# Moving the low parts of the Strassen-stage weights from GpSimd to VectorE

## The chip, the cores and the metric

The kernel runs on one core of one Trainium2 chip. The metric is the device time of one execution in microseconds. Engine names in the rows: PE is TensorE (PEld its weight loads), DVE is VectorE, ACT is ScalarE, POOL is GpSimd, SP is SyncE, which issues nearly all DMAs.

## The reference, cut to what matters

One encoder block on a sequence of 1024 tokens of width 1024: a normalisation, one wide projection `h @ w_in` into twelve parts, a gated three-tap convolution mixer, a bidirectional delta-rule mixer, two gates, two output projections, a residual and a final normalisation. The change touches the part that computes five of the projected parts and multiplies them up:

```
proj = h @ w_in[l]
(a_bg, a_cg, a_x, a_z, q, k, v, z_b, a_raw, b_raw, gate_a_raw, gate_b_raw) = split(proj)
ya = a_cg * dwconv_centred(a_bg * a_x, conv_a_w[l])
ya = ya * jax.nn.silu(a_z)
...
merged = jax.nn.sigmoid(gate_a_raw) * ya + jax.nn.sigmoid(gate_b_raw) * yb
```

## The kernel before, in words

All large products are made in two parts: each float32 operand is written as a high part `hi` (rounded to TensorE's fast 32-bit type) and a low part `lo = x - hi`, and a product is hi·hi + hi·lo + lo·hi, three matmuls where one would do.

The stage of interest makes `a_bg`, `a_x`, `a_cg`, `a_z` (tiles named bg, ax, cg, az) and one pair of column blocks of gate b (gb). It takes the weight columns in pairs of 128-wide blocks, in the order bg, ax, cg, az, four times over, and then gb: 17 pairs. Each pair is a two-by-two block product done with seven products in place of eight (Strassen's scheme in Winograd's form). The seven are named by their weight operand: A11, A12, A22 are weight blocks as they were loaded (tiles `wr_...`), S1 to S4 are sums or differences of blocks (tiles `S_...`). One product is one **step** of the loop: 12 matmuls of 128x512. There are 17 × 7 = 119 steps, in the order S2, A11, S1, S3, A12, A22, S4 for all pairs but the first and the last.

Weights are prepared `AHEAD` = 5 steps before their product. `prep` (line 1203) makes the sum if there is one (VectorE, line 1194, behind the four DMA loads of the pair, line 1199, when it is the pair's first), then the high part (ScalarE, line 1206, tiles `whi..`, `wh..`), then the low part (GpSimd, line 1207, tiles `wlo..`, `wl..`). They go into six slots that are used in turn.

Behind each product stands `after`: VectorE and ScalarE take partial results out of PSUM. Three names matter. `e` is ScalarE's copy of the A11 product (line 1228). `u` (line 1230, VectorE) is the sum of a PSUM bank and `e`; it comes twice in a pair. The bank of pool `pg` first collects S2; the first `u` reads it behind A11, and only then may S3 be added into the same bank, so TensorE has one step (S1) between A11 and the product that waits. The second `u` reads the bank behind S3, and A22 is added only after it, with A12 between. In the first and the last pair the order differs, and A22 stands right behind S3.

In az pairs VectorE also multiplies the results up (line 1302 by c, line 1303 into `a`, between them ScalarE's silu of line 1294); the finished `a` is stored by SyncE (line 1305), behind which the loads of the next ax pair stand in SyncE's queue. In ax pairs line 1296 multiplies into `xpad`, and `conv3` (lines 1313 and 1315) runs the three taps, one a step.

Every engine works off its instructions in the order in which this code is written; an instruction that waits holds up all behind it on its engine.

Of the kernel before, what the change touches and what calls it, by code (L numbers as in the profile page):

```python
# [8 lines left out]
F32 = mybir.dt.float32  # L9
F32R = mybir.dt.float32r  # L10
AF = mybir.ActivationFunctionType
ALU = mybir.AluOpType
# [17 lines left out]
AHEAD = 5  # L30
# [278 lines left out]
def block(ctx: ExitStack, tc: tile.TileContext, x, c, wada, wadag, badaT, nwT, win, wab, cva, cvq,  # L309
# [3 lines left out]
    V, S, G, Q = (Engine(sched, n, e) for n, e in (("dve", nc.vector), ("act", nc.scalar), ("pool", nc.gpsimd),  # L313
                                                   ("dma", nc.sync)))
# [32 lines left out]
    def ch(c, w=P):  # L347
        return slice(w * c, w * c + w)
# [756 lines left out]
    V, S, G, Q, PE = nc.vector, nc.scalar, nc.gpsimd, nc.sync, nc.tensor  # L1105

    def bank(pl, name):
        return pl.tile([P, 512], F32, tag="b", name=name)
# [11 lines left out]
    def product(w, mhi, mlo, half, name, order=tuple(range(KT))):  # L1120
        ps = bank((pp, pg)[half], f"pp_{name}_{half}")
        for i, k in enumerate(order):
            wh, wl = (t[:, ch(i)] for t in w)
            sl = ch(half, 512)
            PE.matmul(ps, wh, mhi[k][:, sl], start=i == 0, stop=False)  # L1125
            PE.matmul(ps, wh, mlo[k][:, sl], start=False, stop=False)  # L1126
            PE.matmul(ps, wl, mhi[k][:, sl], start=False, stop=i == KT - 1)  # L1127
        return ps
# [38 lines left out]
    def slots(name):  # L1167

        i, place[0] = place[0], (place[0] + 1) % 6
        if i > 3:  # L1170
            return [bw.tile([P, 512], F32R, tag=p, name=f"w{p}{name}", bufs=2) for p in "hl"]
        if i % 2 == 0 or not spare:
            spare[:] = [wp.tile([P, KT * P], F32R, tag=f"w{p}", name=f"w{p}{name}") for p in ("hi", "lo")]
        return [t[:, ch(i % 2, 512)] for t in spare]

    class Pair:
# [26 lines left out]
        def prep(self, n):  # L1203
            t = self.operand(n if n in ADDS else (int(n[1]) - 1, int(n[2]) - 1))
            hi, lo = slots(f"{n}_{self.name}")
            S.activation(hi, t, AF.Copy)
            G.tensor_tensor(lo, t, hi.bitcast(F32), ALU.subtract)
            self.ops[n] = hi, lo

        def product(self, n):  # L1210
            own = (self.place, n) in (("first", "S4"), ("last", "A12"), ("last", "S4"))
            pl = po if own else BANK[n]
            first = own or pl not in self.banks
            if first:
                self.banks[pl] = bank(pl, f"ps_{self.name}_{n}")
            ps = self.banks[pl]
            hi, lo = self.ops.pop(n)
            for m in range(4):
                mh, ml = hop[RHS[n]][m]
                for i, (w, r) in enumerate(((hi, mh), (hi, ml), (lo, mh))):  # L1220
                    PE.matmul(ps, w[:, ch(m)], r, start=first and m == i == 0, stop=m == 3 and i == 2,  # L1221
                              skip_group_check=True)
            self.after(n, ps)
# [86 lines left out]
    def conv3(acc, b, j, i):  # L1310
        x, c = xpads[b][:, 1 + i : 1 + i + T], cva_t[:, j, i : i + 1]
        if i:
            V.scalar_tensor_tensor(acc, x, c, acc, ALU.mult, ALU.add)
        else:
            V.tensor_scalar(acc, x, c, None, ALU.mult)
# [21 lines left out]
    steps = [(p, n) for p in pairs for n in p.order]  # L1337

    def gate_block(j, w):
        xp = xpads[j % 2]  # L1340
        for half in range(2):
            ps = product(w, hhi, hlo, half, f"gb{j}", KORDER)
            S.activation(xp[:, 2 + 512 * half : 514 + 512 * half], ps, AF.Sigmoid)
        Q.dma_start(sgb_d[j], xp[:, 2 : T + 2])
# [3 lines left out]
    for i, j in enumerate(plain):  # L1348
        sums(i)
        if j + 1 in plain:  # L1350
            ws.append(wtile(win[G_B + j + 1], f"gb{j + 1}"))
        else:
            for p, n in steps[:4]:
                p.prep(n)
        gate_block(j, ws[i])
    for p, n in steps[4:AHEAD]:
        p.prep(n)
    hctx2.close()
    bt = sctx.enter_context(tc.tile_pool(name="bt", bufs=1, reuse_waits="tile"))
    for i, (p, n) in enumerate(steps):  # L1360
        if i + AHEAD < len(steps):
            q, k = steps[i + AHEAD]
            q.prep(k)
        p.product(n)
        if late:
            conv3(*late.pop(0))
        if i + 4 == len(steps):
            tctx.close()
            yp = ctx.enter_context(tc.tile_pool(name="yp", bufs=1, reuse_waits="tile", side="right"))
            yhi = [yp.tile([P, T], F32R, name=f"yhi{k}") for k in range(KT)]  # L1370
            ylo = [yp.tile([P, T], F32R, name=f"ylo{k}") for k in range(KT)]
            ws = [wtile(win[G_B + j], f"gb{j}") for j in (6, 7)]
            for k in range(KT):
                Q.dma_start(ylo[k].bitcast(F32), y_d[k])
# [204 lines left out]
```

## Time and profile before

| | |
|---|---|
| median of 3 runs | 1456.3 us (1455.89 to 1461.06) |
| the profiled execution: its own time | 1455.84 us |
| its span, first to last instruction | 1453.7 us (2.1 us lie around it) |
| TensorE busy over the span | 1379.9 us (95%) |
| VectorE, ScalarE, GpSimd busy | 828.2, 601.4, 664.9 us (57%, 41%, 46%) |
| mean granted TensorE clock | 0.986 |

How to read it: TensorE is busy for all but 5% of the span, so what another engine does counts where TensorE waits for it. The stage of pairs runs from about 824 to 1160 us of the span.

### The profile page before, as it was taken

What the parts mean: (1) busy time and instruction counts of PE and PEld (TensorE: products, weight loads), DVE (VectorE), ACT (ScalarE), POOL (GpSimd) and SP (SyncE); (2) the same over time, 40 slices, a digit from 0 to 9 for tenths busy, and PEclk for the clock granted to TensorE, in tenths of its full rate; (3) what the DMA queues carried; (4) which work ended last, traced back from release to release, by engine and by line L of the source; (5) the groups of instructions that cost most, each with busy time, mean ns of one, the idle gap of its engine ahead of it and who ended that gap; (6) DMA issues with size and microseconds to landing.
All of it is one profiled execution on the core that took longest, in us unless ns stands there. A gap on an engine that the chain in (4) does not pass through costs nothing.

```text
span 1453.7 us, 22475 instructions
## 1 busy us (share of the span) xinstructions
PE 1379.9 (95%) x8510; PEld 1151.7 (79%) x8510; DVE 828.2 (57%) x1377; ACT 601.4 (41%) x1487; POOL 664.9 (46%) x847
## 2 busy tenths in 40 slices
PE   6999979899989998999799999999999999999998
PEld 5777868787878787887688878787877788888886
DVE  7677165576666766677325556565657545422235
ACT  5437538474546474644443423232232342222211
POOL 2014736663936374757315644455445413355301
PEclk9999999999999999999899999999999999999999
DMA  9233341405050423314112410303030377665402
GB/s 366 75 109 98 99 105 44 131 30 147 15 153 22 107 69 80 96 34 113 44 44 88 145 55 18 116 16 116 29 116 30 123 273 256 207 203 179 179 15 101
DMA packets 123726, 154.41 MB, mean 106 GB/s; under 512 B 74593, under 2 KB 74977, under 8 KB 123618
## 3 DMA queue, kind: packets, MB, share of 16 engines
q1 hardware_dynamic: 123330, 152.19, 33.1%
q8 instruction: 67, 1.10, 0.3%
q10 hardware_dynamic: 288, 0.79, 0.1%
q14 instruction: 41, 0.34, 0.1%
HBM read 123.45 MB, written 29.50 MB: 105 GB/s over the span
## 4 chain that ended last, share of the span: by engine, by line
PE 68%; DVE 11%; DMA 7%; ACT 5%; POOL 4%; issue 3%; SPq 2%; POOLq 0%; ACTq 0%; DVEq 0%
PE cb L210 5%; PE pp_ga L210 5%; PE pp_v L210 4%; PE pp_z L210 3%; PE ps_ax_S L1221 3%; PE o L210 3%; PE ps_cg_S L1221 3%; PE ps_bg_S L1221 3%; PE pp_q L210 3%; PE ps_az_S L1221 2%; DVE N L303 2%; PE pp_pb L1125 2%; PE pp_pb L1127 2%; PE pp_pa L1127 2%; PE pp_pa L1125 2%
## 5 line engine op out<-in xcount | busy, mean ns | idle before, releaser
L303 POOL TENSOR_TENSOR E<-E,et 128x30 f32<-128x30 f32 (+7 forms) x240 | 116.7, 486 | 17.4
L303 POOL TENSOR_TENSOR et<-E 128x30 f32<-128x30 f32 (+7 forms) x240 | 111.3, 464 | 27.9 <-DMA E<-s 11.1
L303 DVE SCALAR_TENSOR_TENSOR S<-S,exps,cb 128x128 f32<-128x128 f32 x96 | 29.8, 344 | 60.2 <-PE cb L210 59.2
L303 ACT ACTIVATE vw<-cb,cols 128x128 f32<-128x128 f32 x112 | 36.2, 364 | 57.3 <-PE cb L210 57.1
L1117 POOL TENSOR_TENSOR wl_pa<-wr_pa,wh_pa 128x512 fp32r<-128x512 f32 x16 | 27.2, 1718 | 70.2 <-ACT wh_pa L1116 55.7
L303 POOL TENSOR_TENSOR wl_ga<-wr_ga,wh_ga 128x512 fp32r<-128x512 f32 x16 | 21.2, 1328 | 79.2 <-ACT wh_ga L303 60.1
L210 PE MATMUL pp_ga<-hhi,wh_ga 128*128 128x512 f32 x128 | 51.8, 404 | 3.4 <-ACT xpad L303 3.4
L303 POOL TENSOR_TENSOR wl_q<-wr_q,wh_q 128x512 fp32r<-128x512 f32 x14 | 18.2, 1304 | 78.8 <-ACT wh_q L303 78.8
L210 PE MATMUL pp_z<-hhi,wl_z 128*128 128x512 f32 x128 | 53.0, 414 | 0.0
L210 PE MATMUL pp_z<-hhi,wh_z 128*128 128x512 f32 x128 | 53.0, 414 | 0.0
L210 PE MATMUL pp_z<-hlo,wh_z 128*128 128x512 f32 x128 | 52.6, 411 | 0.0
L210 PE MATMUL pp_ga<-hhi,wl_ga 128*128 128x512 f32 x128 | 52.2, 408 | 0.0
L210 PE MATMUL pp_ga<-hlo,wh_ga 128*128 128x512 f32 x128 | 51.7, 404 | 0.0
L303 DVE SCALAR_TENSOR_TENSOR r<-cb,negeg,vp 128x128 f32<-128x128 f32 x112 | 34.6, 345 | 29.0 <-PE cb L210 28.2
L1125 PE MATMUL pp_pb<-bhi,wh_pb 128*128 128x512 f32 x128 | 50.4, 394 | 0.0
L1127 PE MATMUL pp_pb<-bhi,wl_pb 128*128 128x512 f32 x128 | 50.2, 392 | 0.0
L1126 PE MATMUL pp_pa<-ylo,wh_pa 128*128 128x512 f32 x128 | 49.8, 389 | 0.0
L1127 PE MATMUL pp_pa<-yhi,wl_pa 128*128 128x512 f32 x128 | 49.8, 389 | 0.0
L1125 PE MATMUL pp_pa<-yhi,wh_pa 128*128 128x512 f32 x128 | 49.8, 389 | 0.0
L1126 PE MATMUL pp_pb<-blo,wh_pb 128*128 128x512 f32 x128 | 49.7, 388 | 0.0
L303 DVE SCALAR_TENSOR_TENSOR qT<-xpad,cvq_t,qT 128x1024 f32<-128x1024 f32 x32 | 46.4, 1450 | 0.4
L210 PE MATMUL pp_v<-hhi,wh_v 128*128 128x512 f32 x112 | 46.4, 414 | 0.0
(802 smaller groups left out, 4603.2 us busy)
## 6 DMA issues: line engine op xcount, KB each, us to landing
wada<-in_wada SPq DMA_DIRECT2D x16, 512.0 KB, 8.9
D<-gr_d SPq DMA_DIRECT2D x16, 512.0 KB, 7.1
xt<-in_x SPq DMA_DIRECT2D x8, 512.0 KB, 9.0
wr_k<-in_win SPq DMA_DIRECT2D x16, 256.0 KB, 2.6
wr_q<-in_win SPq DMA_DIRECT2D x16, 256.0 KB, 3.7
wr_v<-in_win SPq DMA_DIRECT2D x16, 256.0 KB, 3.4
wr_ga<-in_win SPq DMA_DIRECT2D x16, 256.0 KB, 3.3
qg<-er_d SPq DMA_DIRECT2D x8, 512.0 KB, 6.5
```

What stands on the lines that cost most here:

```text
L210: getattr(self.pe, what)(out, *ins, **kw)
L303: self._sched.record(self._name, lambda: real(*args, **kw), outs, ins, cost, extra, table, op == "memset", port)
L1117: G.tensor_tensor(lo[:, ch(q, 512)], raw, hi[:, ch(q, 512)].bitcast(F32), ALU.subtract)
L1125: PE.matmul(ps, wh, mhi[k][:, sl], start=i == 0, stop=False)
L1126: PE.matmul(ps, wh, mlo[k][:, sl], start=False, stop=False)
L1127: PE.matmul(ps, wl, mhi[k][:, sl], start=False, stop=i == KT - 1)
L1221: PE.matmul(ps, w[:, ch(m)], r, start=first and m == i == 0, stop=m == 3 and i == 2, skip_group_check=True)
```

## The change: what it does

`prep` no longer makes the low part. A new method `rest` makes it on VectorE, with the same operands, and is called one step later than `prep` of the same operand: at step i the loop first prepares step i + 5 and then calls `rest` for step i + 4, ahead of the product of step i.

```diff
             S.activation(hi, t, AF.Copy)
-            G.tensor_tensor(lo, t, hi.bitcast(F32), ALU.subtract)
-            self.ops[n] = hi, lo
+            self.ops[n] = hi, lo, t
+
+        def rest(self, n):
+            hi, lo, t = self.ops[n]
+            V.tensor_tensor(lo, t, hi.bitcast(F32), ALU.subtract)
...
-            hi, lo = self.ops.pop(n)
+            hi, lo, _ = self.ops.pop(n)
...
-            for p, n in steps[:4]:
+            for s, (p, n) in enumerate(steps[:4]):
                 p.prep(n)
+                if s:
+                    steps[s - 1][0].rest(steps[s - 1][1])
         gate_block(j, ws[i])
-    for p, n in steps[4:AHEAD]:
-        p.prep(n)
+    for i in range(4, AHEAD):
+        steps[i][0].prep(steps[i][1])
+        steps[i - 1][0].rest(steps[i - 1][1])
...
         if i + AHEAD < len(steps):
             q, k = steps[i + AHEAD]
             q.prep(k)
+        if i + AHEAD <= len(steps):
+            q, k = steps[i + AHEAD - 1]
+            q.rest(k)
         p.product(n)
```

VectorE's queue between the second `u` of an az pair and the first `u` of the bg pair behind it, before (the second of the three places where az is followed by bg looks the same but for numbers; this is the third):

```order
L1230 TENSOR_TENSOR u_az_10064<-ps_az_S_9985,e_az_10017 128x512
L1291 TENSOR_TENSOR t_az_10066<-ps_az_S_10035,u_az_10064 128x512
L1302 TENSOR_TENSOR t_az_10066<-t_az_10066,c_9926 128x512
L1303 TENSOR_TENSOR a_9817<-t_az_10066,a_9817 128x512
L1302 TENSOR_TENSOR t_az_10085<-t_az_10085,c_9945 128x512
L1303 TENSOR_TENSOR a_9836<-t_az_10085,a_9836 128x512
L1194 TENSOR_TENSOR S_bg_10089<-wr_bg_10025,wr_bg_10021 128x512
L1291 TENSOR_TENSOR t_az_10107<-ps_az_S_9985,e_az_10017 128x512
```

The same place in the changed kernel, up to the same instruction, two rows longer:

```order
L1233 TENSOR_TENSOR u_az_10063<-ps_az_S_9984,e_az_10016 128x512
L1294 TENSOR_TENSOR t_az_10065<-ps_az_S_10034,u_az_10063 128x512
L1305 TENSOR_TENSOR t_az_10065<-t_az_10065,c_9925 128x512
L1306 TENSOR_TENSOR a_9816<-t_az_10065,a_9816 128x512
L1211 TENSOR_TENSOR wloA_bg_10048<-wr_bg_10024,whiA_bg_10047 128x512
L1305 TENSOR_TENSOR t_az_10084<-t_az_10084,c_9944 128x512
L1306 TENSOR_TENSOR a_9835<-t_az_10084,a_9835 128x512
L1194 TENSOR_TENSOR S_bg_10088<-wr_bg_10024,wr_bg_10020 128x512
L1211 TENSOR_TENSOR wloA_bg_10048<-S_bg_10028,whiA_bg_10047 128x512
L1294 TENSOR_TENSOR t_az_10106<-ps_az_S_9984,e_az_10016 128x512
```

The rest of that stretch in the changed kernel, up to the first `u` of bg and on to the second one:

```order
L1305 TENSOR_TENSOR t_az_10106<-t_az_10106,c_9925 128x512
L1306 TENSOR_TENSOR a_9816<-t_az_10106,a_9816 128x512
L1211 TENSOR_TENSOR wlS_bg_10091<-S_bg_10088,whS_bg_10090 128x512
L1294 TENSOR_TENSOR t_az_10128<-ps_az_S_10034,u_az_10018 128x512
L1305 TENSOR_TENSOR t_az_10128<-t_az_10128,c_9944 128x512
L1306 TENSOR_TENSOR a_9835<-t_az_10128,a_9835 128x512
L1211 TENSOR_TENSOR wlA_bg_10113<-wr_bg_10026,whA_bg_10112 128x512
L1194 TENSOR_TENSOR S_bg_10151<-wr_bg_10026,S_bg_10030 128x512
L1211 TENSOR_TENSOR wloA_bg_10135<-wr_bg_10022,whiA_bg_10134 128x512
L1233 TENSOR_TENSOR u_bg_10170<-ps_bg_S_10138,e_bg_10168 128x512
L1194 TENSOR_TENSOR S_ax_10180<-wr_ax_10172,wr_ax_10174 128x512
L1194 TENSOR_TENSOR S_ax_10182<-S_ax_10180,wr_ax_10176 128x512
```

Behind these stand two more low parts and then the second `u`, which before the change followed the two sums of ax directly:

```order
L1211 TENSOR_TENSOR wloA_bg_10135<-S_bg_10151,whiA_bg_10134 128x512
L1211 TENSOR_TENSOR wloS_ax_10185<-S_ax_10182,whiS_ax_10184 128x512
L1233 TENSOR_TENSOR u_bg_10215<-ps_bg_S_10138,e_bg_10168 128x512
L1288 TENSOR_TENSOR xpad_116<-ps_bg_S_10188,u_bg_10215 128x512
L1211 TENSOR_TENSOR wloS_ax_10185<-wr_ax_10176,whiS_ax_10184 128x512
```

What moved: 119 rows of line 1207 left GpSimd's queue and stand, as line 1211, in VectorE's, seven to a pair. In the stretch shown five of them come between the second `u` of az and the first `u` of bg (four ahead of the sum `S_bg_10151`, one behind it), and two between the sums of ax and the second `u` of bg. Apart from these, the order on TensorE and ScalarE is as before; on SyncE one store and one load behind the stage change places.

## Rows read from the trace of the kernel before

**Rows 1.** Busy time of the engines in the stage (819 to 1150 us): start and end, length, busy time (instructions) of PE, PEld, DVE, ACT, POOL; then TensorE's granted clock, DMA share, GB/s. The second row is the same for the instructions of line 1207 alone, all of them on POOL.

```profile
819.00:1150.00 331.00, 326.26 (x1406) 262.73 (x1405) 203.29 (x222) 95.45 (x164) 166.46 (x120) 1.00 0.20 67
819.00:1150.00 331.00, 166.09 (x119) 1.00 0.20 67
```

**Rows 2.** TensorE's timeline at the places in the stage where it stood still: start us, duration us, engine, line, operation, out<-in, and in brackets the idle time before it with what ended it. Matmuls overlap, so their starts, not their durations, give the pace.

```profile
841.49 0.47 PE L1221 MATMUL ps_bg_S<-T4h,whiS_bg 128*128 128x512 f32 x1 [0.88 <-DVE u_bg L1230]
...
872.55 0.50 PE L1221 MATMUL ps_cg_S<-T3h,whiS_cg 128*128 128x512 f32 x1 [0.33 <-DVE u_cg L1230]
...
911.12 0.39 PE L1221 MATMUL ps_bg_S<-T1h,wloA_bg 128*128 128x512 f32 x1
912.38 0.50 PE L1221 MATMUL ps_bg_S<-T3h,whiS_bg 128*128 128x512 f32 x1 [0.88 <-DVE u_bg L1230]
912.72 0.39 PE L1221 MATMUL ps_bg_S<-T3l,whiS_bg 128*128 128x512 f32 x1
...
990.66 0.51 PE L1221 MATMUL ps_bg_S<-T3h,whiS_bg 128*128 128x512 f32 x1 [0.47 <-DVE u_bg L1230]
...
996.06 0.40 PE L1221 MATMUL ps_bg_A<-hhi,wloS_bg 128*128 128x512 f32 x1
996.48 0.53 PE L1221 MATMUL ps_bg_S<-T4h,whiA_bg 128*128 128x512 f32 x1
996.84 0.40 PE L1221 MATMUL ps_bg_S<-T4l,whiA_bg 128*128 128x512 f32 x1
...
1069.23 0.50 PE L1221 MATMUL ps_bg_S<-T3h,whS_bg 128*128 128x512 f32 x1 [0.45 <-DVE u_bg L1230]
...
1108.68 0.50 PE L1221 MATMUL ps_cg_S<-T3h,whiS_cg 128*128 128x512 f32 x1 [0.34 <-DVE u_cg L1230]
...
1145.50 0.50 PE L1221 MATMUL ps_gb_S<-T3h,whiS_gb 128*128 128x512 f32 x1 [0.68 <-ACT u_gb L1228]
...
1149.22 0.50 PE L1221 MATMUL ps_gb_S<-T4h,whiA_gb 128*128 128x512 f32 x1 [0.69 <-ACT u_gb L1228]
```

**Rows 3.** VectorE's timeline from the second `u` of an az pair to the first `u` of the bg pair behind it; columns as in rows 2.

```profile
1052.16 0.69 DVE L1230 TENSOR_TENSOR u_az<-ps_az_S,e_az 128x512 f32<-128x512 f32 x1 [2.33 <-PE ps_az_S L1221]
...
1055.00 1.69 DVE L1303 TENSOR_TENSOR a<-t_az,a 128x512 f32<-128x512 f32 x1
...
1057.33 0.69 DVE L1303 TENSOR_TENSOR a<-t_az,a 128x512 f32<-128x512 f32 x1
...
1059.92 1.35 DVE L1302 TENSOR_TENSOR t_az<-t_az,c 128x512 f32<-128x512 f32 x1 [0.70 <-ACT t_az L1294]
1061.31 1.67 DVE L1303 TENSOR_TENSOR a<-t_az,a 128x512 f32<-128x512 f32 x1
...
1065.00 1.70 DVE L1303 TENSOR_TENSOR a<-t_az,a 128x512 f32<-128x512 f32 x1
1066.62 0.68 DVE L1194 TENSOR_TENSOR S_bg<-wr_bg,S_bg 128x512 f32<-128x512 f32 x1
1068.48 0.69 DVE L1230 TENSOR_TENSOR u_bg<-ps_bg_S,e_bg 128x512 f32<-128x512 f32 x1 [1.18 <-ACT e_bg L1228]
```

**Rows 4.** GpSimd's timeline of the same stretch; columns as in rows 2.

```profile
1054.84 1.30 POOL L1207 TENSOR_TENSOR wloA_bg<-S_bg,whiA_bg 128x512 fp32r<-128x512 f32 x1 [0.84 <-ACT whiA_bg L1206]
...
1060.68 1.74 POOL L1207 TENSOR_TENSOR wlA_bg<-wr_bg,whA_bg 128x512 fp32r<-128x512 f32 x1
1064.84 1.31 POOL L1207 TENSOR_TENSOR wloA_bg<-wr_bg,whiA_bg 128x512 fp32r<-128x512 f32 x1 [2.42 <-ACT whiA_bg L1206]
```

**Rows 5.** VectorE's timeline shortly before the stage: two low parts of the same form and size that VectorE makes already, one behind the other; columns as in rows 2.

```profile
816.92 0.68 DVE L1157 TENSOR_TENSOR T1l<-hx,T1h 128x512 fp32r<-128x512 f32 x1
817.52 0.69 DVE L1157 TENSOR_TENSOR T2l<-hx,T2h 128x512 fp32r<-128x512 f32 x1
```

**Rows 6.** VectorE's timeline from the A22 result of an ax pair towards the first `u` of the cg pair behind it: two rows of an earlier ax pair (942.79 and 944.78), then three of the last one; columns as in rows 2.

```profile
942.79 0.75 DVE L1315 TENSOR_SCALAR a<-xpad,cva_t 128x1024 f32<-128x1024 f32 x1
...
944.78 2.60 DVE L1313 SCALAR_TENSOR_TENSOR a<-xpad,cva_t,a 128x1024 f32<-128x1024 f32 x2
...
1098.00 1.66 DVE L1296 TENSOR_TENSOR xpad<-t_ax,xpad 128x512 f32<-128x512 f32 x1
1099.70 1.68 DVE L1315 TENSOR_SCALAR a<-xpad,cva_t 128x1024 f32<-128x1024 f32 x1
...
1102.62 3.53 DVE L1313 SCALAR_TENSOR_TENSOR a<-xpad,cva_t,a 128x1024 f32<-128x1024 f32 x2
```

**Rows 7.** SyncE's queue (two stores of `a`, then the loads of the next ax pair) and VectorE's timeline in front of the second `u` of a bg pair; columns as in rows 2.

```profile
984.44 4.04 SPq L1305 DMA_DIRECT2D y_d<-a  x2
988.53 2.25 SPq L1199 DMA_DIRECT2D wr_ax<-in_win  x4
...
993.23 0.69 DVE L1194 TENSOR_TENSOR S_ax<-wr_ax,wr_ax 128x512 f32<-128x512 f32 x1 [2.63 <-DMA wr_ax<-in_win]
995.13 0.69 DVE L1194 TENSOR_TENSOR S_ax<-S_ax,wr_ax 128x512 f32<-128x512 f32 x1 [1.20 <-DMA wr_ax<-in_win]
995.74 0.68 DVE L1230 TENSOR_TENSOR u_bg<-ps_bg_S,e_bg 128x512 f32<-128x512 f32 x1
```

**Rows 8.** Behind the stage: SyncE's store of the first of two gate blocks, which the loads `wr_pa` stand right behind in its queue, and ScalarE's first use of those loads; columns as in rows 2.

```profile
1172.11 0.32 SPq L1344 DMA_DIRECT2D sgb_d<-xpad  x1
...
1178.22 1.23 ACT L1116 ACTIVATE wh_pa<-wr_pa 128x512 fp32r<-128x512 f32 x2 [6.14 <-DMA wr_pa<-in_wpa]
```

## The prediction, made before the run

> **What bounds the kernel now.** I looked first at the busy shares: TensorE is busy for 95% of the span, so a change on other engines can only give back what TensorE loses by waiting for them. So I next took the busy times of the stage of pairs alone: in 331 us TensorE is busy for 326.3, VectorE for 203.3, ScalarE for 95.5 and GpSimd for 166.5, of which 166.1 are the 119 low parts that the change moves [rows 1]. Two things are to be seen there. GpSimd is not idle in this stage: it is half busy, with just this work, and would be idle after the change. And TensorE loses 4.7 us in the whole stretch, with the granted clock at its full level (1.00) throughout, so neither clock nor load leaves much to win.
>
> The third view is TensorE's own timeline, to find those microseconds. They lie at nine places [rows 2]. Eight name what ended them: six times a `u` on VectorE, twice ScalarE's `u_gb`. The ninth, at 996.48, has no bracket, but its start is late too. What one costs is more than the bracket: at 912.38 the starts lie 911.12, 912.38, 912.72, where an undisturbed pace is 0.23 apart (912.72 to the next, and all through the steps: 12 matmuls take 2.76). That is 1.60 - 0.46 = 1.14 for a bracket of 0.88: 0.26 more for the slow restart. I add 0.26 to each bracket. The places then cost: 841.49, 1.14; 872.55, 0.59; 912.38, 1.14; 990.66, 0.73; 996.48, 0.78 - 0.46 = 0.32 from its three starts; 1069.23, 0.71; 1108.68, 0.60; 1145.50, 0.94; 1149.22, 0.95. Together 7.1 us, 0.49% of the time: the ceiling of any gain here.
>
> Two of them cannot close. In the first and the last pair A22 stands right behind S3 in the same bank, so `u` must fit between two neighbouring products whatever else runs: 841.49 and 1149.22 stay, 2.1 us. What can be won is 5.0 us.
>
> **The change part by part.** *Removed:* 119 GpSimd instructions of 1.30 us, up to 1.74 where VectorE runs against them [rows 4]. GpSimd is waited for nowhere among the nine places, so their going is worth nothing by itself.
>
> *Removed with them: collisions.* VectorE's line 1303 takes 0.69 us at 1057.33, when GpSimd does nothing, and 1.69, 1.67 and 1.70 at 1055.00, 1061.31 and 1065.00 [rows 3], each started while a low part ran on GpSimd (1054.84, 1060.68, 1064.84) [rows 4]. The first ran until 1056.14 on GpSimd, and VectorE's ended 0.55 later, at 1056.69: it waits until GpSimd is through and then runs. So a hit costs VectorE 1.0 us. Line 1302 at 1059.92 took 1.35, 0.66 more than its 0.69 kin. In this stretch, from the second `u` of az at 1052.16 to the first `u` of bg at 1068.48, that is 3 × 1.0 + 0.66 = 3.7 us that go when GpSimd is silent. I take all of it, since the short and the long form of the same instruction stand beside each other; the bound from below is none of it.
>
> *Added:* 119 low parts on VectorE. The nearest row is the same form a little earlier, 0.68 us, with starts 0.60 apart when two stand in a row [rows 5]; I take 0.60. That is 71 us more work. With no collision saved VectorE would go from 203 to 275 of 331 us, still under TensorE; so what counts is not the load but how late a `u` comes. In the stretch shown five low parts come between the two `u`. The last lies between the sum S_bg and `u`, where VectorE stood idle for 1.18 us while ScalarE first made the high part and then `e` [rows 3]: free. If that wait shrank to nothing it would cost 0.60. The other four cost 2.4 us. So `u` comes 3.7 - 2.4 = 1.3 us earlier. It was late by 0.71, 0.73 and 1.14 at the three places of this kind (1069.23, 990.66, 912.38), so all three close: **-2.6 us.**
>
> *The two cg places* (872.55 and 1108.68). Behind the A22 result of ax, for which VectorE waits, its rows to the S4 sum hold collisions of 1.66 - 0.69 = 0.97 (line 1296, against the 0.69 of the same form) and about 0.9 each in lines 1315 and 1313, whose 1.68 and 3.53 stand against 0.75 and 2.60 in an earlier pair [rows 6]: 2.8 saved, two low parts or 1.2 added. `u_cg` comes 1.6 earlier and was 0.6 late: **-1.2 us.**
>
> *gb* (1145.50). ScalarE's `u_gb` stands behind a silu that waits for VectorE at the end of the last az; of the collisions in front of it I count 2.7 us (lines 1302, 1303, 1303) against 1.2 for two low parts: 1.5 earlier, 0.94 late: **-0.9 us.**
>
> *The second `u` of bg* gets worse by order. Two low parts now stand ahead of it, behind two sums that wait for the DMA loads of ax [rows 7]. The second of them needs ScalarE's high part of the sum just made, so `u` follows that sum by 0.69 + 0.66 + 0.69, some 2.0, where it followed in 0.61: 1.4 later. The loads themselves stand in SyncE's queue right behind the stores of `a` (4.04 us for two, then 2.25 for four loads) [rows 7], and the last `a` is the end of az's work, which comes 3.7 - 1.8 (three low parts) = 1.9 earlier. So `u` comes about 0.5 earlier in all, but TensorE is there 0.7 to 1.1 earlier too, its own gap before it being closed. The gap of 0.32 at 996.48 becomes about 0.6, and its two sister places, which had 0.3 to 0.9 to spare, come to about nothing: **+0.3 us.**
>
> *Supply.* A low part is now asked for one step later, but still four products of 2.76 us ahead of its use; VectorE is at most some 4 us behind, so TensorE does not wait for it. A low part may wait for ScalarE's high part and hold up VectorE; the sum of the next step stands ahead of it and the `u` behind it needs a later product anyway, except at the place just priced.
>
> *Behind the stage* no waiting takes the gain back: the loads `wr_pa` stand behind the store of a gate block that TensorE itself has just finished, and ScalarE, which waits for them, starts 6.1 us behind that store [rows 8]; all of it shifts with TensorE.
>
> The sum: -2.6 - 1.2 - 0.9 + 0.3 = -4.4 us on the profiled execution's 1455.84 (span 1453.7 and 2.1 around it): 1451.4. The median of the runs lies 0.5 above that execution, so I say **1451.9 us** for the median, -0.3%.
>
> **The rivals.**
> *Given back at the second `u`.* If the stores and loads of ax do not come earlier (4 us pass between issue and the first sum, and DMA times scatter), each of the three bg pairs loses up to 1.4 us at the second `u`, 4.2 less what two of them have to spare (0.3 and 0.9, from which TensorE's earlier arrival takes most): about 3.5. Then -4.7 + 3.5: 1454 to 1456, no difference. For it speaks that VectorE waited 2.63 and 1.20 us for just these loads [rows 7]; against it, that they follow the stores at once.
>
> *VectorE becomes late: slower.* If the long forms of lines 1302, 1303, 1313 do not shorten, the four low parts ahead of `u_bg` cost 2.4 us three times, two ahead of `u_cg` 1.2 four times, gb 1.2 and the second `u` 1.4 three times: 7.2 + 4.8 + 1.2 + 4.2 = 17 us, 1473. It decides from the point where the stretch saves less than the 2.4 us that it pays, that is under 0.6 us for each long row. The pairs of long and short rows speak against it. The Trainium skill, Perfetto Trace Analysis, section on optimizing Scalar/DVE operations, advises the opposite of this change, to offload VectorE to GpSimd where VectorE is saturated; by that rule this rival holds. The trace has VectorE at 61% in the stage, not saturated, and the same section warns that the two share an SBUF read port so that offloading may not help, which the 1.69 against 0.69 bear out.
>
> *All gaps close but the two inherent ones and something more comes free:* at most -7.1, 1449.2. Nothing in the profile gives more.
>
> That the low parts do not move is excluded by the order of the instructions.
>
> **How the numbers follow.** A measurement of this kernel tells about 0.5% (7 us) from no change. Forecast (1450 to 1453.5): 0.57. Given back (1454 to 1457): 0.25. VectorE late in part or whole (1458 to 1473): 0.12. More than counted (under 1449.5): 0.06. The first two lie within 0.5%; of the slow case two thirds pass 1463.6, of the last half pass 1449.0: faster 0.03, same 0.89, slower 0.08. The range leaves out most of the slow case and half of the last: 1449 to 1459; the likeliest case's own is 1450 to 1453.5.
>
> **What would show it.** In the changed kernel's profile: line 1303 at 0.69 throughout and GpSimd near zero in the stage; VectorE above its 203 us but clearly under the 275 of no saved collision; TensorE's brackets at the `u_cg`, first `u_bg` and first `u_gb` places gone, two left in the first and last pair, one of about 0.6 at the second `u_bg`. Wrong I would be if line 1303 stayed near 1.7 with GpSimd silent, if `u_bg` waited for loads that came no earlier, or if a matmul on a `wlo` tile waited for line 1211.

## The result, and the profile after

| | before | after |
|---|---|---|
| median, first comparison (6 runs each) | 1457.28 us | 1450.17 us |
| ratio, 95% interval | | 0.9949 (0.9925 to 0.9974) |
| median, second comparison (29 and 12 runs) | 1456.44 us | 1450.85 us |
| ratio, 95% interval | | 0.9967 (0.9953 to 0.9981) |
| the profiled execution: its time, its span | 1455.84, 1453.7 us | 1447.78, 1446.0 us |
| VectorE, GpSimd busy over the span | 828.2, 664.9 us | 856.7, 497.3 us |

The change makes the kernel faster by 0.3% (0.2 to 0.5%), some 5 us; the forecast was -4.4 us and 1451.9. It is a small gain, about what a single comparison can just tell, so the traces carry the argument from here.

The busy times of the changed kernel's stage (819 to 1150 us; columns as in [rows 1]):

```profile
819.00:1150.00 331.00, 328.98 (x1425) 266.84 (x1424) 226.06 (x338) 99.27 (x169) 4.69 (x4) 1.00 0.21 72
```

Against [rows 1], GpSimd fell from 166.46 to 4.69 us. VectorE rose by only 22.8 us although it does about 116 more instructions in the window: at a pace of 0.60 us they are 70 us, so some 47 us of waiting went out of VectorE's other instructions.

One difference between the two profiled executions is no part of the effect. To take it out, two landmarks are read in each trace: TensorE's first matmul of the gate-b product ahead of the stage (`pp_gb`) and its first one behind the stage (`pp_pa`). First before, then after:

```profile
779.96 0.39 PE L1125 MATMUL pp_gb<-hhi,wh_gb 128*128 128x512 f32 x1
1182.27 0.39 PE L1125 MATMUL pp_pa<-yhi,wh_pa 128*128 128x512 f32 x1
```

```profile
776.59 0.39 PE L1125 MATMUL pp_gb<-hhi,wh_gb 128*128 128x512 f32 x1
1174.55 0.39 PE L1125 MATMUL pp_pa<-yhi,wh_pa 128*128 128x512 f32 x1
```

From one landmark to the other it is 402.3 us before and 398.0 after: 4.3 us. This is called the **stretch** below. The other 3.4 us lie ahead of it, in code that is the same in both kernels: in the executions profiled later the first landmark lies at 782.5 for the kernel before and 781.9 for the changed one, and between 777.9 and 783.4 over all variants. So that part is taken as scatter from one execution to the next. The two ratios of the table can't be told apart either: their intervals overlap.

TensorE's timeline after, at the places where its starts lie further apart than 0.23 (columns as in [rows 2]):

```profile
838.19 0.47 PE L1224 MATMUL ps_bg_S<-T4h,whiS_bg 128*128 128x512 f32 x1 [0.95 <-DVE u_bg L1233]
...
912.75 0.40 PE L1224 MATMUL ps_bg_A<-hhi,wloS_bg 128*128 128x512 f32 x1
913.54 0.50 PE L1224 MATMUL ps_bg_S<-T4h,whA_bg 128*128 128x512 f32 x1 [0.39 <-DVE u_bg L1233]
913.88 0.39 PE L1224 MATMUL ps_bg_S<-T4l,whA_bg 128*128 128x512 f32 x1
...
1068.64 0.50 PE L1224 MATMUL ps_bg_S<-T4h,whiA_bg 128*128 128x512 f32 x1
...
1141.50 0.50 PE L1224 MATMUL ps_gb_S<-T4h,whiA_gb 128*128 128x512 f32 x1 [0.69 <-ACT u_gb L1231]
```

Of the nine places of [rows 2] two are left in the first and the last pair (838.19 and 1141.50), and the only other ones are second `u` of bg: 913.54, which costs 913.88 - 912.75 - 0.46 = 0.67, and 1068.64, which costs 0.17. All first `u` of bg, both `u_cg` and the first `u_gb` are gone from the list. The sum is 3.0 us where it was 7.1.

VectorE's timeline after, from the second `u` of az to the first `u` of bg, the stretch of [rows 3]:

```profile
1046.56 0.69 DVE L1233 TENSOR_TENSOR u_az<-ps_az_S,e_az 128x512 f32<-128x512 f32 x1 [1.11 <-PE ps_az_S L1224]
...
1049.40 0.69 DVE L1306 TENSOR_TENSOR a<-t_az,a 128x512 f32<-128x512 f32 x1
1050.01 0.68 DVE L1211 TENSOR_TENSOR wloA_bg<-wr_bg,whiA_bg 128x512 fp32r<-128x512 f32 x1
...
1055.26 0.69 DVE L1306 TENSOR_TENSOR a<-t_az,a 128x512 f32<-128x512 f32 x1
...
1058.58 0.69 DVE L1306 TENSOR_TENSOR a<-t_az,a 128x512 f32<-128x512 f32 x1
...
1060.39 0.69 DVE L1211 TENSOR_TENSOR wloA_bg<-wr_bg,whiA_bg 128x512 fp32r<-128x512 f32 x1
1061.66 0.69 DVE L1233 TENSOR_TENSOR u_bg<-ps_bg_S,e_bg 128x512 f32<-128x512 f32 x1 [0.58 <-ACT e_bg L1231]
```

The products into `a` take 0.69 where they took 1.69, 1.67 and 1.70. From `u` to `u` it is 15.10 us, against 1068.48 - 1052.16 = 16.32 in [rows 3]: 1.22 earlier, with five more instructions in between. The fifth low part was hidden as expected: the wait for ScalarE's `e` ahead of `u_bg` shrank from 1.18 to 0.58. The same over the whole stage, VectorE's instructions by line, with count, busy time and mean ns; first before, then after:

```profile
L1303 DVE TENSOR_TENSOR a<-t_az,a 128x512 f32<-128x512 f32 x16 | 23.0, 1435 | 0.5
L1296 DVE TENSOR_TENSOR xpad<-t_ax,xpad 128x512 f32<-128x512 f32 x12 | 14.2, 1181 | 0.4
```

```profile
L1306 DVE TENSOR_TENSOR a<-t_az,a 128x512 f32<-128x512 f32 x16 | 11.1, 692 | 0.5
...
L1299 DVE TENSOR_TENSOR xpad<-t_ax,xpad 128x512 f32<-128x512 f32 x12 | 8.3, 693 | 0.4
```

### The profile page after: what moved, and what is told of

It reads as the page before. It is cut to its first block, busy times and chain, and to the rows that moved or that the text cites. A ratio compares the mean times of both kernels' runs of the same rounds, so it can differ in the third digit from the quotient of the medians.

```text
span 1446.0 us, 22411 instructions
## 1 busy us (share of the span) xinstructions
PE 1375.5 (95%) x8510; PEld 1150.6 (80%) x8510; DVE 856.7 (59%) x1496; ACT 601.9 (42%) x1487; POOL 497.3 (34%) x728
## 4 chain that ended last, share of the span: by engine, by line
PE 71%; DVE 9%; POOL 6%; DMA 5%; ACT 4%; issue 3%; SPq 2%; POOLq 0%; ACTq 0%; DVEq 0%
PE pp_ga L210 5%; PE cb L210 4%; PE ps_cg_S L1224 4%; PE ps_ax_S L1224 4%; PE pp_v L210 4%; PE ps_az_S L1224 3%; PE ps_bg_S L1224 3%; PE o L210 3%; PE pp_z L210 3%; DVE N L303 3%; PE pp_q L210 3%; POOL E L303 2%; PE pp_pb L1125 2%; PE pp_pb L1127 2%; PE pp_pa L1127 2%
## 5 line engine op out<-in xcount | busy, mean ns | idle before, releaser
L1117 POOL TENSOR_TENSOR wl_gb<-wr_gb,wh_gb 128x512 fp32r<-128x512 f32 x12 | 17.9, 1510 | 337.0 <-PE ps_gb_S L1224 326.6
```

Source lines behind the costliest of these rows:

```text
L1117: G.tensor_tensor(lo[:, ch(q, 512)], raw, hi[:, ch(q, 512)].bitcast(F32), ALU.subtract)
```

## The experiments

The theory: the change gains by what GpSimd stops doing. Its low parts made VectorE's instructions wait (collisions), this made `u` late, and TensorE waited for `u`. VectorE pays for the moved work, but less than the collisions had cost it. The rivals: GpSimd's silence is worth nothing and the gain is scatter; or the loads of ax, or something else behind the stage, decide. All variants are read by the time and by the stretch between the two landmarks.

### The two kernels again

Both unchanged, to separate the stage from the scatter ahead of it.

> The kernel before, unchanged, run and profiled again. Theory A (the change saves some 4 us inside the stage, by nine gaps of TensorE that shrink from 7.1 to 3.0 us; the other 3 us between the two first profiles lie ahead of the stage, where nothing was changed, and are scatter): the first matmul of pp_gb, 780.0 us in the first profile of before, lies elsewhere this time, by some microseconds, and the nine gaps are there again with 7 us together. Theory B (the change also speeds up the part ahead of the stage, by a way not yet seen): that matmul lies at 780 again, within 1 us.

> The changed kernel, unchanged, run and profiled again. Theory A: ratio to before 0.996 to 0.998 (4 to 5 us), the stretch from the first matmul of pp_gb to the first of pp_pa 397.9 us again (402.3 before), and the first matmul of pp_gb not always earlier than in before. Theory B: ratio 0.994 to 0.996 and that matmul at 776.6 within 1 us.

Measured: the kernel before 1457.47 us, ratio to itself 1.0007 (0.9994 to 1.002); the changed one 1450.85, ratio 0.9967 (0.9953 to 0.9981). The stretch is 402.2 before and 398.9 after. So the kernel before has the same nine places in a second execution and the same stretch within 0.1; the changed one varies by 0.9, where the expectation had 397.9 again. That difference lies in the second `u` of bg. TensorE's timeline of this second execution of the changed kernel at two of them:

```profile
918.02 0.40 PE L1224 MATMUL ps_bg_A<-hhi,wloS_bg 128*128 128x512 f32 x1
919.09 0.50 PE L1224 MATMUL ps_bg_S<-T4h,whA_bg 128*128 128x512 f32 x1 [0.67 <-DVE u_bg L1233]
919.43 0.40 PE L1224 MATMUL ps_bg_S<-T4l,whA_bg 128*128 128x512 f32 x1
...
997.22 0.53 PE L1224 MATMUL ps_bg_S<-T4h,whiA_bg 128*128 128x512 f32 x1 [0.30 <-DVE u_bg L1233]
```

By the three starts the first costs 1.41 - 0.46 = 0.95, and by the same working the second 0.60 and a third at 1074.82 0.15: 1.7 us in all, where the first profile had 0.84.

### GpSimd's work back, VectorE's kept

Two variants of the changed kernel in which GpSimd makes each low part as well. In the first (the first diff) it writes the same tile that VectorE then writes; in the second it writes a tile that nothing reads.

```diff
             S.activation(hi, t, AF.Copy)
+            G.tensor_tensor(lo, t, hi.bitcast(F32), ALU.subtract)
             self.ops[n] = hi, lo, t
```

```diff
             S.activation(hi, t, AF.Copy)
+            idle = bw.tile([P, 512], F32, tag="idle", name=f"x{n}_{self.name}", bufs=1)
+            G.tensor_tensor(idle, t, hi.bitcast(F32), ALU.subtract)
             self.ops[n] = hi, lo, t
```

> The changed kernel in which GpSimd also makes each low part, where it did before, so that VectorE's work stays added and the collisions come back. Theory (what pays for the added work is that GpSimd no longer holds VectorE up): lines 1306 and 1316 go back to some 1.7 and 2.3 us where they meet a low part on GpSimd, first u of bg and cg come 1 to 3 us later than before the change, the stage grows by 10 to 20 us over that of before: 1465 to 1477. Rival (the collisions cost nothing that counts, the gap closes because the low parts are ready earlier or the order is better): as the changed kernel, 1448 to 1454.

> The changed kernel, and beside it GpSimd makes each low part too, into a tile that nothing reads, so VectorE waits for GpSimd nowhere. Collisions are back and VectorE's 119 low parts stay. My theory (the gain comes from the collisions that vanish, and pays for VectorE's added work): line 1209's neighbours, the products into `a`, go from 0.69 back to a mean near 1.4 us, low parts on VectorE to 0.8 to 1.2, and the stretch from the first gate-b product of pairs to the first product behind the stage goes from 398 to between 412 and 428 us, 1466 to 1480 in all; less than the 441.6 of the run with two makers of one tile, as far as there VectorE waited for GpSimd. Rival one (silence of GpSimd does nothing, VectorE has room anyway): as the change, 398, 1451. Rival two (the wait for GpSimd's copy was nothing in that run, collisions were all): 438 to 442, 1490 to 1496.

Measured: the first 1495.67 us, ratio 1.027 (1.024 to 1.03), stretch 441.6; the second 1480.34, ratio 1.0156 (1.0134 to 1.0177), stretch 423.7. What TensorE waited for in the stage, in us in total, times, and the longest, in the first variant and then in the second:

```profile
PE ps_bg_S L1225 <- DVE u_bg L1234: 19.0, 7, 3.6
PE ps_cg_S L1225 <- DVE u_cg L1234: 12.9, 8, 1.7
```

```profile
PE ps_bg_S L1226 <- DVE u_bg L1235: 11.6, 6, 3.1
PE ps_cg_S L1226 <- DVE u_cg L1235: 8.5, 8, 1.8
PE ps_gb_S L1226 <- ACT u_gb L1233: 2.8, 2, 2.0
```

VectorE's timeline in the second variant at the first of the three places, the second `u` of az, three of the four products into `a`, and the first `u` of bg:

```profile
897.24 0.69 DVE L1235 TENSOR_TENSOR u_az<-ps_az_S,e_az 128x512 f32<-128x512 f32 x1 [1.36 <-PE ps_az_S L1226]
...
900.40 1.74 DVE L1308 TENSOR_TENSOR a<-t_az,a 128x512 f32<-128x512 f32 x1
...
907.43 1.66 DVE L1308 TENSOR_TENSOR a<-t_az,a 128x512 f32<-128x512 f32 x1
...
911.72 1.74 DVE L1308 TENSOR_TENSOR a<-t_az,a 128x512 f32<-128x512 f32 x1
...
915.92 0.69 DVE L1235 TENSOR_TENSOR u_bg<-ps_bg_S,e_bg 128x512 f32<-128x512 f32 x1 [0.66 <-ACT e_bg L1233]
```

The second variant is the clean one: VectorE waits for GpSimd in no dependency, all its work is that of the changed kernel, and yet 11 of the 16 products into `a` take 1.66 us or more (median 1.67) and the stretch grows by 25 to 26 us. That GpSimd subtracts beside it is enough. The stretch falls inside what the theory gave (412 to 428); silence without effect would have left 398.

GpSimd's reading could also act by another way: ScalarE waits for it four times in this stage, 7.2 us in all, before it can write a high part. The rows leave no room for that at this place. From `u` to `u` it is 18.68 us, against 15.50 in the change: 3.18 later. The three long products make 1.05 + 0.97 + 1.05 = 3.07 of it, and a row of line 1307 that took 0.83 instead of 0.69 makes 0.14. So the whole delay stands in VectorE's own longer rows.

The first variant missed its expectation, which put it far lower. Of the 18 us between the two, some 4.5 are TensorE's clock: in four stretches of the first variant the granted clock was 0.50 to 0.57, and 32 spaces between matmuls took some 6 us more than at full level, against 1.6 us more in the second variant. The rest comes with a wait that the first adds: VectorE's low part must stand until GpSimd's copy into the same tile is written.

```profile
L1212 DVE TENSOR_TENSOR wloS_ax<-S_ax,whiS_ax 128x512 fp32r<-128x512 f32 x10 | 11.1, 1112 | 3.5 <-POOL wloS_ax L1207 3.5
```

This row of the first variant (ten instructions, 3.5 us of VectorE's idle time ended by GpSimd) is one of several such; all of VectorE's low parts together waited 34.5 us for GpSimd.

### Neither GpSimd's work nor VectorE's

The kernel before, with the subtraction left out: ScalarE writes a second rounded copy where the low part should be.

```diff
-            G.tensor_tensor(lo, t, hi.bitcast(F32), ALU.subtract)
+            S.activation(lo, t, AF.Copy)
```

> The kernel before, with the low part replaced by a second rounded copy of the operand on ScalarE (the subtraction is left out, so the output is not the reference's): GpSimd is silent and VectorE gets no work added, ScalarE gets about 119 x 0.65 = 77 us. My theory (collisions make the lateness of `u`): all first and second `u` of bg and the `u` of cg come in time, the places in the first and the last pair stay at about 1.1 each, and the stretch is 396.5 to 397.8, some 1 us under the change, 1449 to 1451 in all. Rival (ScalarE's `e` and `u_gb` come late behind the added copies): the gaps at `u_gb` stay or grow and new ones appear behind `e`, 399 to 403.

Measured: 1452.31 us, ratio 0.9964 (0.9951 to 0.9978), stretch 397.05. The stage's busy row, and all that TensorE waited for in it:

```profile
819.00:1150.00 331.00, 329.37 (x1429) 267.69 (x1429) 160.34 (x226) 159.11 (x288) 3.87 (x3) 1.00 0.21 71
```

```profile
PE ps_bg_S L1221 <- DVE u_bg L1230: 0.9, 1, 0.9
PE ps_gb_S L1221 <- ACT u_gb L1228: 0.7, 1, 0.7
```

Only the places in the first and the last pair are left, and the stretch is as expected; the time lies 1.3 us over the expected 1449 to 1451. The stretch is 5.2 us under the kernel before; the prediction had counted 5.0 that could be won at all, so the excess of the seven other places is now measured by itself. ScalarE's 64 us more cost nothing. VectorE is busy for 160.3 us here against 203.3 in [rows 1], with all but the same work (222 and 226 instructions): the collisions cost it some 43 us in the stage.

With this the four cases stand side by side (stretch in us):

| | GpSimd silent in the stage | GpSimd subtracts |
|---|---|---|
| VectorE without low parts | 397.1 | 402.3 (before) |
| VectorE with 119 low parts | 398.0 and 398.9 (after) | 423.7 |

The collisions alone cost 5.2 us, the added work alone 0.9 to 1.8, and both together 26.6 (1.6 of them TensorE's lower clock, as the last section shows). They don't add up, because TensorE sees only the part of a delay that exceeds what each `u` has to spare.

### The low part in the same step as the high part

The kernel before with one letter changed: VectorE makes the low part at once, without the step of delay.

```diff
-            G.tensor_tensor(lo, t, hi.bitcast(F32), ALU.subtract)
+            V.tensor_tensor(lo, t, hi.bitcast(F32), ALU.subtract)
```

> Low parts on VectorE, as in the change, but asked for in the same step as the high part, right behind it, not one step later. GpSimd is silent in both. If the delay of one step matters, VectorE stands at each low part until ScalarE has made the high part (ScalarE 0.65 and the hand-over, about 0.8 us where ScalarE is free, more behind an `e`): about 7 such waits a pair, idle time named by ScalarE's tiles up to 60 to 90 us, some `u` late by 0.5 to 1.5, stretch 399 to 406, 1452 to 1459 in all. Rival (VectorE is idle a third of the time, so where it waits is immaterial): as the change, 398, 1451.

Measured: 1458.96 us, ratio 1.0019 (0.9999 to 1.0038), stretch 406.1: 7 to 8 us behind the change, and no better than before. VectorE's waits in the stage (the first two and one more of 14 such lines), and what TensorE waited for in turn:

```profile
DVE wloS_ax L1207 <- ACT whiS_ax L1206: 15.9, 11, 4.1
DVE wloS_az L1207 <- ACT whiS_az L1206: 12.2, 9, 4.1
...
DVE wloA_ax L1207 <- ACT whiA_ax L1206: 7.8, 3, 2.9
```

```profile
PE ps_bg_S L1221 <- DVE u_bg L1230: 6.2, 7, 1.4
```

GpSimd is as silent as in the change and the products into `a` take 0.69 us here too, but VectorE stands at low parts, up to 4.1 us where ScalarE itself stands at an `e`. In the changed kernel such waits add up to 3.4 us: one of 2.1, and seven of 0.2 or less. All such waits of this variant come to 76 us, inside the expected 60 to 90, and the stretch lies at the upper end of what was expected. So the step of delay is worth more than the whole gain: moving the work without it would have given the gain back.

### The order of low part and product

Three variants of the changed kernel in which `rest` comes behind the product of the step and its `u`: in every step, in the steps of S3, and in the S3 step of bg pairs alone.

The first:

```diff
+        p.product(n)
         if i + AHEAD <= len(steps):
             q, k = steps[i + AHEAD - 1]
             q.rest(k)
-        p.product(n)
```

The third; the second has the same with `n == "S3"` alone as the condition:

```diff
+        behind = n == "S3" and p.name.startswith("bg")
+        if behind:
+            p.product(n)
         if i + AHEAD <= len(steps):
             q, k = steps[i + AHEAD - 1]
             q.rest(k)
-        p.product(n)
+        if not behind:
+            p.product(n)
```

> The changed kernel with the call of rest moved behind product, so that the low parts stand behind the partial sums u in VectorE's queue. If the low parts ahead of the second u of bg are what is left of TensorE's gaps there (0.67 us at 913.5 and 0.17 at 1068.6 in the changed kernel), these close and the stage is 0.8 us shorter, the time the same as that of the changed kernel within what can be told. If instead the late loads of ax alone hold that u, the two gaps stay. If the low parts come too late for TensorE there, matmuls on a wlo tile show waits for VectorE and the time grows by more than 2 us.

> The changed kernel, but in the step of S3, behind which the second `u` stands, the low part comes behind the product and its `u` instead of ahead of it; all other steps as in the change. If the 0.2 to 0.7 us left at the second `u` of bg come from the low part that waits there for ScalarE, these gaps go and, other than with all low parts behind the product, the first `u` of bg does not get a fifth low part ahead of it and shows no new gap: stretch 397.0 to 397.8, 1449.5 to 1450.5 in all, not to be told from the change by time. Rival (the loads of ax set the second `u`): gaps there as in the change, 398 to 399.

> The changed kernel, but the low part comes behind the product in one step of a pair only: that of S3 in the bg pairs, where it stands ahead of the second `u`. At S3 of az the order is that of the change, so the stretch between the second `u` of az and the first `u` of bg keeps its four low parts ahead of the sum. If the two gaps that the changes of order traded against each other are set by the count of low parts ahead of each `u`, both close: nothing but the places of the first and the last pair is left (about 1.1 each), and the stretch is 397.0 to 397.4, what the run without low parts on VectorE and GpSimd had, 1449.5 to 1450.5 in all. Rival (the loads of ax set the second `u` by themselves): 0.2 to 0.7 left at one of the three places, 397.5 to 398.5. Neither can be told from the change by the time.

Measured: 1450.85, 1451.42 and 1451.95 us, ratios 0.997 (0.9955 to 0.9985), 0.9961 (0.9946 to 0.9977) and 0.9966 (0.9952 to 0.998): none to be told from the change. Stretches: 397.8, 397.8 and 397.1. The stretches of the second and the third lie inside what was expected of them, their times 0.9 and 1.5 us over it. In the first two variants the gaps at the second `u` close, but a first `u` of bg is late, in the second by the same amount as in the first. TensorE's timeline of the first:

```profile
909.96 0.50 PE L1224 MATMUL ps_bg_S<-T3h,whiS_bg 128*128 128x512 f32 x1 [0.23 <-DVE u_bg L1233]
```

Neither expectation had this, and so the first variant did not bring the 0.8 us that was expected of it. In the second variant the cause is one of order: the second `u` of az stands behind an S3 as well, so the low part that goes behind that product falls into the stretch to the first `u` of bg, which gets a fifth low part ahead of its wait. From `u` to `u` it is 16.09 us there and 16.10 in the first variant, against 15.50 at this place in the change: one low part of 0.60. The third variant leaves az alone, and what TensorE waited for is

```profile
PE ps_bg_S L1224 <- DVE u_bg L1233: 0.9, 1, 0.9
PE ps_gb_S L1224 <- ACT u_gb L1231: 0.7, 1, 0.7
```

the two places of the first and the last pair alone, with the same stretch as the variant without any low part on VectorE. The loads of ax were no faster there (5.72 to 6.42 us from issue to second sum); the second `u` of bg follows that sum by 1.21 us, where it is 2.06 to 2.08 in the change. All that the stage has to give is had with this order; over the change it is 0.9 to 1.8 us, less than the times can show.

### GpSimd busy without reading

The changed kernel, in which GpSimd fills an unused tile with zeros twice a step.

```diff
             S.activation(hi, t, AF.Copy)
+            if marks:
+                S.activation(tiny, marks.pop()[:, 0:1], AF.Copy)
+            idle = bw.tile([P, 512], F32, tag="idle", name=f"x{n}_{self.name}", bufs=1)
+            G.memset(idle, 0.0)
+            G.memset(idle, 0.0)
+            marks.append(idle)
```

> The changed kernel, and GpSimd fills a tile that nothing needs with zeros twice in every step (119 x 2 instructions of 128x512 that write and read nothing; one column of it is copied on ScalarE in each step, so that the fills go step by step and not all at once, some 0.2 us each or 24 us in the stage). If what blocks VectorE is that GpSimd reads its operands, as VectorE's rows with two SBUF operands do, the products into `a` stay at 0.69 and the stretch at 398 to 399, 1450 to 1452 in all (up to 1 more if `e` comes late behind the added copies). Rival (any work of GpSimd on SBUF blocks): the products into `a` go above 1.0 in the mean, and the stretch gets 5 to 20 us longer, 1456 to 1471.

The expectation's words "write and read nothing" are wrong in one half: the fills write their tile, and read nothing. Measured: 1452.1 us, ratio 0.9974 (0.9961 to 0.9988), stretch 398.3. The copies on ScalarE took half of the 24 us that were expected (busy 112.10 against 99.27). The stage's busy row, VectorE's products into `a`, and then one fill and one product that started beside it:

```profile
819.00:1150.00 331.00, 328.97 (x1424) 266.89 (x1423) 227.83 (x340) 112.10 (x284) 127.65 (x239) 1.00 0.20 69
```

```profile
L1315 DVE TENSOR_TENSOR a<-t_az,a 128x512 f32<-128x512 f32 x16 | 11.1, 692 | 0.5
```

```profile
903.24 0.53 POOL L1213 MEMSET xA_bg<- 128x512 f32 x1 [0.56 <-ACT tiny L1211]
```

```profile
903.33 0.69 DVE L1315 TENSOR_TENSOR a<-t_az,a 128x512 f32<-128x512 f32 x1
```

GpSimd is busy for 127.65 us, 12 of the 16 products ran beside a fill for most of their time, and all 16 took 0.69. So neither GpSimd's being busy nor its writing is what blocks these rows. What the fills lack, against the subtractions, is above all the reading of operands; that it is the reading is the explanation that fits, not one that a run with reading alone has shown.

## Why the prediction was right

*The ceiling and the two places that cannot close.* Right. The variant without low parts on either engine gave back 5.2 us of the counted 5.0, and the places of the first and the last pair stayed in every variant.

*The collisions.* Right: with GpSimd silent line 1306 takes 0.69 us in all its 16 instructions, and with GpSimd subtracting beside the same VectorE work 1.67 in the median. How late `u` comes follows these rows to 0.1 us, in the change and in the clean variant of the second experiment. The Trainium skill, SBUF — State Buffer, section "Who interferes with whom", has the rule behind it: a VectorE instruction with two operands in SBUF contends with a GpSimd instruction that reads SBUF, and the loser blocks fully. The trace agrees on both halves: subtractions on GpSimd lengthen these rows by 1.0 us and fills don't. The prediction cited another page's warning of the same sharing (the Trainium skill, Perfetto Trace Analysis, on optimizing Scalar/DVE operations); that page's advice to move work to GpSimd is for a saturated VectorE, and at the 61% of [rows 1] the opposite move gained.

*The three first `u` of bg.* Right in mechanism and size: 1.3 earlier was forecast, 1.22 measured at the third place, 1.25 at the first; all three places closed.

*cg and gb.* Right in mechanism and size: the two `u_cg` places and the first `u_gb` are gone. Counted from the `u` ahead of it, `u_cg` comes 1.7 us earlier at both places (forecast 1.6), and the first `u_gb` 1.5 earlier (forecast 1.5).

*The second `u` of bg.* The mechanism held, the term was too small: +0.3 was forecast, and 0.84 - 0.32 = +0.5 was measured in one execution and 1.7 - 0.32 = +1.4 in the other. Two parts of the working held at all three places and in both executions. The loads of ax are issued 1.8 to 1.9 us earlier (13.1 to 13.4 us behind the second `u` of az, where it was 14.9 to 15.3; forecast 1.9). And `u` follows the second sum by 2.06 to 2.08 us (forecast "some 2.0"). VectorE's and SyncE's rows after, at the first place:

```profile
904.43 2.26 SPq L1199 DMA_DIRECT2D wr_ax<-in_win  x4
```

```profile
910.72 0.69 DVE L1194 TENSOR_TENSOR S_ax<-S_ax,wr_ax 128x512 f32<-128x512 f32 x1 [0.23 <-DMA wr_ax<-in_win]
911.33 0.68 DVE L1211 TENSOR_TENSOR wlS_bg<-S_bg,whS_bg 128x512 fp32r<-128x512 f32 x1
912.19 0.69 DVE L1211 TENSOR_TENSOR wloS_ax<-S_ax,whiS_ax 128x512 fp32r<-128x512 f32 x1 [0.18 <-ACT whiS_ax L1206]
912.80 0.68 DVE L1233 TENSOR_TENSOR u_bg<-ps_bg_S,e_bg 128x512 f32<-128x512 f32 x1
```

The step that failed is "So `u` comes about 0.5 earlier in all": it took the time from the issue of the loads to the second sum to be the same before and after. In two executions of each kernel it is, in us:

| | first place | second place | third place |
|---|---|---|---|
| before | 5.81, 6.08 | 6.60, 6.52 | 6.29, 5.40 |
| after | 6.29, 6.56 | 5.63, 6.52 | 6.15, 6.14 |

So the loads scatter by 1.2 us within the kernel before alone, and they are not slower after the change (6.1 in the mean before, 6.2 after). With this scatter the second `u` came 0.3 earlier in the mean of the three places, not 0.5: 0.1 later at the first place, where TensorE was there 1.1 earlier and the largest gap is left, and 1.4 earlier at the second place of the first execution, where none is. How large the term comes out in one execution is then in part luck. This is the rival "given back at the second `u`" in a small part: its scattering loads came true, its loads that come no earlier did not, and its 3.5 us were not reached. Why the loads scatter is open; no run took that apart.

*The sum.* Forecast -4.4; the stretch gave -4.3 and -3.3, the times -4.8 us (-6.8 to -2.8). The median was forecast at 1451.9 and came at 1450.2 and 1450.9. Some 0.3 us of the difference in time lies outside the span, where the prediction took 2.1 us for both kernels: 2.0 to 2.2 us lie around it in the executions of the kernel before, 1.7 to 1.8 in those of the changed one. Why is open.

*The rival "VectorE becomes late"* was priced at +17 us for the case that the long rows stay long. The variant in which they do stay long measured +21.4 in the stretch, some 1.6 of it by TensorE's lower clock: it was a sound price for a condition that doesn't hold.

*A step without a number.* The prediction said that a low part that waits for ScalarE does little harm. True with the step of delay; but that delay, taken for granted, is what the gain hangs on, 7 to 8 us as the fourth experiment shows.

## What to carry to other kernels

An engine that nobody waits for can still be the cause of a wait: look for one form of instruction with two durations, and for what ran on GpSimd while the long ones did. Moving such work onto the blocked engine can pay even though that engine gets busier in total, if what remains ahead of each awaited result is less than the collisions that go. Place the moved work behind what it needs, not at the point where it was asked for before, and count how many instructions stand ahead of each result that TensorE waits for.

## What the runs showed of the hardware beyond that

Only some forms of VectorE are blocked. In the kernel before, rows with one operand in PSUM and one in SBUF stay short while those with two in SBUF do not; and one form with a single SBUF operand is blocked too. VectorE's instructions of the stage by line (count, busy time, mean ns):

```profile
L1315 DVE TENSOR_SCALAR a<-xpad,cva_t 128x1024 f32<-128x1024 f32 x8 | 9.0, 1120 | 0.1
...
L1230 DVE TENSOR_TENSOR u_az<-ps_az_S,e_az 128x512 f32<-128x512 f32 x8 | 5.5, 692 | 26.1 <-ACT e_az L1228 15.8 <-PE ps_az_S L1221 10.3
```

`u` has a mean of 692 ns in both kernels, although most of these rows ran beside a low part on GpSimd before the change. The scaling of `xpad` takes 1120 before and 748 after, for 1024 columns where the others do 512. By the Trainium skill, on the same page and section as above, a form that runs in a mode with two ports takes the shared pair as well; 748 ns for twice the columns fits such a mode. The run with fills fits it too: there this form does meet GpSimd. One scaling that began at 940.76, during a fill that ran from 940.65 to 941.18, took 0.96 us, and a fill that began during a scaling took 0.72 in place of 0.53. The fills are short, so the mean rises to 776 ns only.

A collision costs by where it falls: 43 us of VectorE's time in the stage for 166 us of GpSimd's, of which TensorE saw 5.2.

In the clean variant of the second experiment TensorE's matmuls lay 0.43 apart instead of 0.23 from 1001.1 to 1004.1 us, behind a wait of 2.42 us for `u_bg` that ended at 1000.25. The busy row of 1000 to 1005 us:

```profile
1000.00:1005.00 5.00, 4.75 (x14) 3.78 (x15) 2.98 (x6) 1.15 (x2) 1.17 (x2) 0.66 0.97 359
```

The granted clock is 0.66 here and 1.00 in the five microseconds on either side, so TensorE ran at its lower level (1.2 GHz) for about 3 us: nine spaces between matmuls took 3.65 us where 2.07 is the pace, so some 1.6 of the 25 to 26 us are the clock. Behind the other waits of 2.5 to 3.1 us in that trace it didn't happen. In the first variant of that experiment it happened behind waits of 3.57, 3.06, 3.56 and 2.04 us for `u_bg` and not behind those of 2.69 and 2.58, so the length of one wait alone doesn't tell.
